# Row sums joined by 32x32 transposes on VectorE in place of products on TensorE, in a log-softmax over eight 25 KB buffers

## Chip, cores, metric

One core of one Trainium2 chip. The metric is device time in microseconds of one execution. All runs quoted here are on record as of the fast state, with a granted clock of 1.0.

## The reference

```python
# x: (16, 512, 50000) float32
max_x = np.max(x, axis=-1, keepdims=True)
shifted = x - max_x
log_sum_exp = np.log(np.sum(np.exp(shifted), axis=-1, keepdims=True))
return (shifted - log_sum_exp).astype(np.float32)
```

## The kernel before

A tile is 16 rows. Each row is cut into G = 8 pieces of 6250 numbers, one piece per partition, so a tile is 128 x 6250 float32: 25 KB per partition, 3125 KB in all. There are 512 tiles and eight buffers, used in turn. Since a row lies on eight partitions, its maximum and its sum have to be joined over those eight. The maximum was already joined by two 32x32 transposes on VectorE; the sum was joined on TensorE, by a product with a block matrix of ones.

```python
# SyncE: load tile into buffer j when the store from it is done
take(sync, stored[j])
sync.dma_start(out=bufs[j], in_=dram(xq, q, j)).then_inc(landed[j], 16)

# VectorE, per tile: front(j), then back(j - 1)
def front(j):
    take(vector, landed[j])
    vector.reduce_max(out=pmax, in_=bufs[j], axis=AX)            # 128x6250
    # transpose, reduce over groups of 8, spread, transpose back -> shift[j]
    ...
def back(j):                                                     # waits for logs[j]
    vector.tensor_scalar(out=bufs[j], in0=bufs[j], scalar1=shift[j][:, 0:1],
                         scalar2=logs[j], op0=ALU.add, op1=ALU.subtract)

# ScalarE, per tile: front(j), then back(j - 1)
def front(j):
    for c in range(nexp):                                        # 2 exponentials, waiting for shift[j]
        scalar.activation(out=dump, ..., func=ACT.Exp, accum_out=parts[j][:, c:c+1])
    added.next(scalar.activation(out=logs[j], in_=rowsum[:, j:j+1], func=ACT.Ln))
def back(q, j):                                                  # waits for the subtract of j
    subtracted.next(scalar.dma_start(out=dram(oq, q, j), in_=bufs[j]))

# TensorE, per tile: both partial sums, joined over the partitions of a row
for c in range(nexp):
    tensor.matmul(rowsum[:, j:j+1], ones, parts[j][:, c:c+1], start=c == 0, stop=c == nexp - 1)
```

(Semaphores are cut here except where a name shows which wait is meant.)

Of the kernel before, what the change touches and what calls it, by code (L numbers as in the profile page):

```python
# [8 lines left out]
FP32 = mybir.dt.float32  # L9
ACT = mybir.ActivationFunctionType  # L10
ALU = mybir.AluOpType
AX = mybir.AxisListType.X

P = 128
SQ = 32

G = 8
R = P // G
# [22 lines left out]
def take(engine, sem):  # L41

    engine.wait_ge(sem, 16).then_inc(sem, -16)  # L43


@with_exitstack
def kernel(
    ctx: ExitStack,
    tc: tile.TileContext,
    x: bass.AP,  # L50
    out: bass.AP,
):
    nc = tc.nc
    xf = x.flatten_outer_dims()
    of = out.flatten_outer_dims()
    N, V = xf.shape
    W = V // G
    assert N % R == 0 and V % G == 0 and W % EXP_C == 0
    ntiles = N // R
    nexp = W // EXP_C  # L60
    assert ntiles % NBUF == 0 and ntiles >= 2 * NBUF

    rounds = ntiles // NBUF
    xq = xf.rearrange("(q j r) (g w) -> q j (r g) w", j=NBUF, r=R, g=G)
    oq = of.rearrange("(q j r) (g w) -> q j (r g) w", j=NBUF, r=R, g=G)

    data = ctx.enter_context(tc.tile_pool(name="data", bufs=1))
    stats = ctx.enter_context(tc.tile_pool(name="stats", bufs=1))
    consts = ctx.enter_context(tc.tile_pool(name="consts", bufs=1))
    dump_pool = ctx.enter_context(  # L70
        tc.tile_pool(name="dump", bufs=1, space=bass.MemoryType.PSUM)
    )
    sum_pool = ctx.enter_context(
        tc.tile_pool(name="sums", bufs=1, space=bass.MemoryType.PSUM)
    )

    ones = consts.tile([P, P], FP32)
    bufs = [data.tile([P, W], FP32, name=f"buf{j}") for j in range(NBUF)]
    shift = [stats.tile([P, SQ], FP32, name=f"negmax{j}") for j in range(NBUF)]
    logs = [stats.tile([P, 1], FP32, name=f"logsum{j}") for j in range(NBUF)]  # L80
    parts = [stats.tile([P, nexp], FP32, name=f"part{j}") for j in range(NBUF)]
    pmax = stats.tile([P, 1], FP32, name="pmax")
    allmax = stats.tile([P, SQ], FP32, name="allmax")
    rowmax = stats.tile([P, SQ // G], FP32, name="rowmax")
    spread = stats.tile([P, SQ], FP32, name="spread")
    dump = dump_pool.tile([P, EXP_C], FP32, name="dump")
    rowsum = sum_pool.tile([P, NBUF], FP32, name="rowsum")


    ctx.enter_context(tc.tile_critical())  # L90

    def sem(name):
        return ctx.enter_context(nc.semaphore(name))

    landed = [sem(f"landed{j}") for j in range(NBUF)]
    stored = [sem(f"stored{j}") for j in range(NBUF)]
    ready = sem("ones_ready")
    on_dve = Count(sem("on_dve"))
    on_act = Count(sem("on_act"))
    shifted = Count(sem("shifted"))  # L100
    summed = Count(sem("summed"))
    added = Count(sem("added"))
    logged = Count(sem("logged"))
    subtracted = Count(sem("subtracted"))


    def dram(a, q, j):
        if isinstance(q, int):
            return a[q, j]
        return a[bass.ds(q, 1), j].rearrange("o p w -> (o p) w")  # L110

    block = ctx.enter_context(nc.Block())

    @block.gpsimd
    def _(gpsimd):

        ones3 = ones.rearrange("p (r g) -> p r g", g=G)
        gpsimd.memset(ones, 1.0).then_inc(ready)  # L118
        gpsimd.affine_select(  # L119
            out=ones3, in_=ones3, pattern=[[-G, R], [0, G]], base=0,  # L120
            channel_multiplier=1, compare_op=ALU.is_ge, fill=0.0,
        ).wait_op(ready, 1, "sem-ge").then_inc(ready)
        gpsimd.affine_select(  # L123
            out=ones3, in_=ones3, pattern=[[G, R], [0, G]], base=G - 1,
            channel_multiplier=-1, compare_op=ALU.is_ge, fill=0.0,
        ).wait_op(ready, 2, "sem-ge").then_inc(ready)

    @block.sync
    def _(sync):
        for j in range(NBUF):  # L130
            sync.dma_start(out=bufs[j], in_=dram(xq, 0, j)).then_inc(landed[j], 16)
        with sync.Fori(1, rounds) as q:
            for j in range(NBUF):
                take(sync, stored[j])
                sync.dma_start(out=bufs[j], in_=dram(xq, q, j)).then_inc(landed[j], 16)
        for j in range(NBUF):
            take(sync, stored[j])

    @block.vector
    def _(vector):  # L140
        def front(j):
            take(vector, landed[j])
            vector.reduce_max(out=pmax, in_=bufs[j], axis=AX).then_inc(on_dve.sem)  # L143

            on_dve.next(
                vector.transpose(out=allmax, in_=pmax.to_broadcast([P, SQ]))  # L146
            ).then_inc(on_dve.sem)
            on_dve.next(
                vector.tensor_reduce(  # L149
                    out=rowmax, in_=allmax.rearrange("p (r g) -> p r g", g=G),  # L150
                    op=ALU.max, axis=AX, negate=True,
                )
            ).then_inc(on_dve.sem)
            on_dve.next(
                vector.tensor_copy(  # L155
                    out=spread.rearrange("p (r g) -> p r g", g=G),
                    in_=rowmax[:, :, None].to_broadcast([P, SQ // G, G]),
                )
            ).then_inc(on_dve.sem)
            on_dve.next(vector.transpose(out=shift[j], in_=spread)).then_inc(shifted.sem)  # L160

        def back(j):
            logged.next(
                vector.tensor_scalar(  # L164
                    out=bufs[j], in0=bufs[j], scalar1=shift[j][:, 0:1], scalar2=logs[j],
                    op0=ALU.add, op1=ALU.subtract,
                )
            ).then_inc(subtracted.sem)

        def settle():  # L170
            on_dve.settle(vector)
            logged.settle(vector)

        for j in range(NBUF):
            front(j)
            if j:
                back(j - 1)
        settle()
        with vector.Fori(1, rounds):
            for j in range(NBUF):  # L180
                front(j)
                back((j - 1) % NBUF)
            settle()
        back(NBUF - 1)

    @block.scalar
    def _(scalar):
        def front(j):
            for c in range(nexp):
                ins = scalar.activation(  # L190
                    out=dump, in_=bufs[j][:, c * EXP_C : (c + 1) * EXP_C], func=ACT.Exp,
                    bias=shift[j][:, 0:1], scale=1.0, accum_out=parts[j][:, c : c + 1],
                )
                (on_act if c else shifted).next(ins)
                ins.then_inc(on_act.sem if c < nexp - 1 else summed.sem)
            added.next(
                scalar.activation(out=logs[j], in_=rowsum[:, j : j + 1], func=ACT.Ln)  # L197
            ).then_inc(logged.sem)

        def back(q, j):  # L200
            subtracted.next(
                scalar.dma_start(out=dram(oq, q, j), in_=bufs[j])
            ).then_inc(stored[j], 16)

        def settle():
            for count in (on_act, shifted, added, subtracted):
                count.settle(scalar)

        nc.scalar.preload_act_table_set("natural_log_exp_and_others")  # L209
        for j in range(NBUF):  # L210
            front(j)
            if j:
                back(0, j - 1)
        settle()
        with scalar.Fori(1, rounds) as q:
            last = q - 1
            for j in range(NBUF):
                front(j)
                back(q if j else last, (j - 1) % NBUF)
            settle()  # L220
        back(rounds - 1, NBUF - 1)

    @block.tensor
    def _(tensor):
        def add(j):
            for c in range(nexp):
                ins = tensor.matmul(  # L227
                    rowsum[:, j : j + 1], ones, parts[j][:, c : c + 1],
                    start=c == 0, stop=c == nexp - 1,
                )  # L230
                if c == 0:
                    summed.next(ins)
            ins.then_inc(added.sem)

        tensor.wait_ge(ready, 3)
        with tensor.Fori(0, rounds):
            for j in range(NBUF):
                add(j)
            summed.settle(tensor)


# [28 lines left out]
```

## Time and profile before

| | before |
|---|---|
| time, median of the 3 runs known at first | 7620.1 us |
| steady period of a tile | 14.87 us |
| bytes moved in the steady part | 432 GB/s |
| VectorE / ScalarE / TensorE busy | 73% / 41% / 7% |
| a load, issue to landing; a store | 51.8 us; 37.0 us |

How to read the page: "DMA" gives the busy share of the 16 DMA engines in 40 equal slices of the run, in tenths, and "GB/s" what they moved in each. A line of a group is: source line, engine, operation, output and inputs, shapes, count | busy us in all, mean ns of one | idle us of that engine just before them, and what ended it. A line of a timeline is: start us, duration us, engine, and so on, with the idle time before it in brackets. The lines themselves, from the page and from one steady cycle, stand in the prediction.

### The profile page before, as it was taken

The page shows a single profiled execution, that of the slowest core. Times are in us where ns is not written, and L with a number is a line of the kernel's source. Part 1 is how long each engine was busy: PE and PEld are TensorE (multiplying, and loading weights), DVE is VectorE, ACT ScalarE, POOL GpSimd, SP SyncE. Part 2 cuts the span into 40 slices and gives each one's busy share as a digit, 9 for nine tenths or more (in the row PEclk, how much of TensorE's full clock was granted, in tenths as well). Part 3 has the DMA queues.
Part 4 walks back from the last instruction along what each step waited for, and adds up shares of the span by engine and source line. Part 5 has one row for each costly group of instructions (what it writes and reads, how often), then busy time and mean ns, then how long its engine had stood idle before and what let it go on. Part 6 is the DMA issues. An engine that isn't in the chain of part 4 may idle for free. (4 is left out here: it accounts for less than half of the span.)

```text
span 7617.7 us, 14954 instructions
## 1 busy us (share of the span) xinstructions
PE 519.0 (7%) x2048; PEld 475.1 (6%) x2048; DVE 5565.8 (73%) x3072; ACT 3153.3 (41%) x2561; POOL 1.2 (0%) x7
## 2 busy tenths in 40 slices
PE   0000000000000000000000000000000000000000
PEld 0000000000000000000000000000000000000000
DVE  7777777777777777777777777777777777777776
ACT  4444444444444444444444444444444444444443
POOL 0000000000000000000000000000000000000000
DMA  9999999999999999999999999999999999999998
GB/s 424 432 433 432 432 432 432 433 432 432 432 433 433 432 432 432 433 432 432 432 432 433 432 432 432 433 433 432 431 432 433 432 432 432 432 432 432 431 430 366
DMA packets 147459, 3276.88 MB, mean 430 GB/s; under 512 B 16385, under 2 KB 16385, under 8 KB 16385
## 3 DMA queue, kind: packets, MB, share of 16 engines
q1 hardware_dynamic: 73728, 1638.43, 50.0%
q10 hardware_dynamic: 73728, 1638.43, 50.0%
q14 instruction: 3, 0.02, 0.0%
HBM read 1638.40 MB, written 1638.40 MB: 430 GB/s over the span
## 5 line engine op out<-in xcount | busy, mean ns | idle before, releaser
L143 DVE TENSOR_REDUCE pmax<-buf 128x1 f32<-128x6250 f32 x512 | 3411.5, 6663 | 1960.6 <-DVEq L43 1960.6
L190 ACT ACTIVATE dump<-buf,negmax 128x3125 f32<-128x3125 f32 x1024 | 2938.2, 2869 | 3878.6 <-DVE negmax L160 3862.1
L164 DVE TENSOR_SCALAR buf<-buf,negmax,logsum 128x6250 f32<-128x6250 f32 x512 | 1789.4, 3495 | 3.9 <-ACT logsum L197 3.9
L227 PE MATMUL rowsum<-part,ones 128*128 128x1 f32 x2048 | 519.0, 357 | 7078.5 <-ACT dump L190 7078.5
L227 PEld LDWEIGHTS rowsum<-part,ones 128*128 128x128 f32 x2048 | 475.1, 322 | 7122.2 <-ACT dump L190 7122.2
L197 ACT ACTIVATE logsum<-rowsum 128x1 f32<-128x1 f32 x512 | 87.6, 171 | 564.8 <-PE rowsum L227 564.8
L190 ACT ACTIVATION_READ_ACCUMULATOR dump<-buf,negmax 128x1 f32 x1024 | 190.8, 186 | 0.0
L160 DVE STREAM_TRANSPOSE negmax<-spread 128x32 f32<-128x32 f32 x512 | 108.3, 212 | 17.7
L146 DVE STREAM_TRANSPOSE allmax<-pmax 128x32 f32<-128x32 f32 x512 | 108.3, 211 | 17.6
L149 DVE TENSOR_REDUCE rowmax<-allmax 128x4 f32<-128x32 f32 x512 | 95.1, 186 | 17.7
L155 DVE COPY spread<-rowmax 128x32 f32<-128x32 f32 x512 | 92.5, 181 | 17.8
L209 ACT ACT_TABLE_LOAD x1 | 1.3, 1283 | 1.0 <-SPq L90 1.0
L119 POOL TENSOR_SCALAR_AFFINE_SELECT ones<-ones 128x128 f32<-128x128 f32 x1 | 0.4, 403 | 0.1
L123 POOL TENSOR_SCALAR_AFFINE_SELECT ones<-ones 128x128 f32<-128x128 f32 x1 | 0.4, 397 | 0.1
L118 POOL MEMSET ones<- 128x128 f32 x1 | 0.2, 204 | 0.5 <-SPq L90 0.5
L254 POOL MEMSET const-bfloat16-1.0<- 128x1 bf16 x1 | 0.1, 101 | 0.0
L254 POOL MEMSET const-uint8-127<- 128x1 uint8 x1 | 0.1, 101 | 0.0
L254 POOL MEMSET const-float32-0.0<- 128x1 f32 x1 | 0.1, 98 | 0.3 <-issue 0.3
L254 POOL MEMSET const-float32-1.0<- 128x1 f32 x1 | 0.1, 98 | 0.0
## 6 DMA issues: line engine op xcount, KB each, us to landing
buf<-in_x_dram SPq DMA_DIRECT2D x512, 3125.0 KB, 51.8
out_dram<-buf ACTq DMA_DIRECT2D x512, 3125.0 KB, 37.0
```

The costliest lines, as they stand in the source:

```text
L119: gpsimd.affine_select(out=ones3, in_=ones3, pattern=[[-G, R], [0, G]], base=0, channel_multiplier=1, compare_op=ALU.is_ge, fill=0.0,).wai ...
L123: gpsimd.affine_select(out=ones3, in_=ones3, pattern=[[G, R], [0, G]], base=G - 1, channel_multiplier=-1, compare_op=ALU.is_ge, fill=0.0,) ...
L143: vector.reduce_max(out=pmax, in_=bufs[j], axis=AX).then_inc(on_dve.sem)
L146: vector.transpose(out=allmax, in_=pmax.to_broadcast([P, SQ]))
L149: vector.tensor_reduce(out=rowmax, in_=allmax.rearrange("p (r g) -> p r g", g=G), op=ALU.max, axis=AX, negate=True,)
L155: vector.tensor_copy(out=spread.rearrange("p (r g) -> p r g", g=G), in_=rowmax[:, :, None].to_broadcast([P, SQ // G, G]),)
L160: on_dve.next(vector.transpose(out=shift[j], in_=spread)).then_inc(shifted.sem)
L164: vector.tensor_scalar(out=bufs[j], in0=bufs[j], scalar1=shift[j][:, 0:1], scalar2=logs[j], op0=ALU.add, op1=ALU.subtract,)
L190: ins = scalar.activation(out=dump, in_=bufs[j][:, c * EXP_C : (c + 1) * EXP_C], func=ACT.Exp, bias=shift[j][:, 0:1], scale=1.0, accum_out ...
L197: scalar.activation(out=logs[j], in_=rowsum[:, j : j + 1], func=ACT.Ln)
L209: nc.scalar.preload_act_table_set("natural_log_exp_and_others")
L227: ins = tensor.matmul(rowsum[:, j : j + 1], ones, parts[j][:, c : c + 1], start=c == 0, stop=c == nexp - 1,)
```

## The change

The intent: the join of the sums leaves TensorE. VectorE adds the two partial sums and sends them through the same four small operations that join the maximum (now a helper, `share`), just before the subtract that needs them. So that ScalarE does not stop for this, its logarithm of tile j-1 is moved ahead of the exponentials of tile j.

```diff
     def _(vector):
-        def front(j):
-            take(vector, landed[j])
-            vector.reduce_max(out=pmax, in_=bufs[j], axis=AX).then_inc(on_dve.sem)
+        def share(out, op, done, negate=False):
             ... (transpose, reduce by groups of 8, spread, transpose back: as before)
+        def front(j):
+            take(vector, landed[j])
+            vector.reduce_max(out=own, in_=bufs[j], axis=AX).then_inc(on_dve.sem)
+            share(shift[j], ALU.max, shifted, negate=True)

         def back(j):
+            summed.next(
+                vector.tensor_reduce(out=own, in_=parts[j], op=ALU.add, axis=AX)
+            ).then_inc(on_dve.sem)
+            share(totals[j], ALU.add, added)
             logged.next(
                 vector.tensor_scalar(
... (ScalarE)
+        def log(j):
             added.next(
-                scalar.activation(out=logs[j], in_=rowsum[:, j : j + 1], func=ACT.Ln)
+                scalar.activation(out=logs[j], in_=totals[j][:, 0:1], func=ACT.Ln)
             ).then_inc(logged.sem)
...
             for j in range(NBUF):
+                log((j - 1) % NBUF)
                 front(j)
                 back(q if j else last, (j - 1) % NBUF)
             settle()
+        log(NBUF - 1)
         back(rounds - 1, NBUF - 1)
-
-    @block.tensor
-    ... (all of it, and GpSimd's making of the matrix of ones)
```

More of the change, by code (lines that the diff above doesn't have):

```diff
@@ L68 @@
     stats = ctx.enter_context(tc.tile_pool(name="stats", bufs=1))
-    consts = ctx.enter_context(tc.tile_pool(name="consts", bufs=1))
     dump_pool = ctx.enter_context(
@@ L72 @@
     )
-    sum_pool = ctx.enter_context(
-        tc.tile_pool(name="sums", bufs=1, space=bass.MemoryType.PSUM)
-    )
-    ones = consts.tile([P, P], FP32)
     bufs = [data.tile([P, W], FP32, name=f"buf{j}") for j in range(NBUF)]
     shift = [stats.tile([P, SQ], FP32, name=f"negmax{j}") for j in range(NBUF)]
+    totals = [stats.tile([P, SQ], FP32, name=f"total{j}") for j in range(NBUF)]
     logs = [stats.tile([P, 1], FP32, name=f"logsum{j}") for j in range(NBUF)]
     parts = [stats.tile([P, nexp], FP32, name=f"part{j}") for j in range(NBUF)]
-    pmax = stats.tile([P, 1], FP32, name="pmax")
-    allmax = stats.tile([P, SQ], FP32, name="allmax")
-    rowmax = stats.tile([P, SQ // G], FP32, name="rowmax")
+    own = stats.tile([P, 1], FP32, name="own")
+    block32 = stats.tile([P, SQ], FP32, name="block32")
+    rowval = stats.tile([P, SQ // G], FP32, name="rowval")
     spread = stats.tile([P, SQ], FP32, name="spread")
     dump = dump_pool.tile([P, EXP_C], FP32, name="dump")
-    rowsum = sum_pool.tile([P, NBUF], FP32, name="rowsum")
     ctx.enter_context(tc.tile_critical())
@@ L96 @@
     stored = [sem(f"stored{j}") for j in range(NBUF)]
-    ready = sem("ones_ready")
     on_dve = Count(sem("on_dve"))
@@ L112 @@
     block = ctx.enter_context(nc.Block())
-    @block.gpsimd
-    def _(gpsimd):
-        ones3 = ones.rearrange("p (r g) -> p r g", g=G)
-        gpsimd.memset(ones, 1.0).then_inc(ready)
-        gpsimd.affine_select(
-            out=ones3, in_=ones3, pattern=[[-G, R], [0, G]], base=0,
-            channel_multiplier=1, compare_op=ALU.is_ge, fill=0.0,
-        ).wait_op(ready, 1, "sem-ge").then_inc(ready)
-        gpsimd.affine_select(
-            out=ones3, in_=ones3, pattern=[[G, R], [0, G]], base=G - 1,
-            channel_multiplier=-1, compare_op=ALU.is_ge, fill=0.0,
-        ).wait_op(ready, 2, "sem-ge").then_inc(ready)
     @block.sync
@@ L140, in _ @@
     def _(vector):
-        def front(j):
-            take(vector, landed[j])
-            vector.reduce_max(out=pmax, in_=bufs[j], axis=AX).then_inc(on_dve.sem)
+        def share(out, op, done, negate=False):
             on_dve.next(
-                vector.transpose(out=allmax, in_=pmax.to_broadcast([P, SQ]))
+                vector.transpose(out=block32, in_=own.to_broadcast([P, SQ]))
             ).then_inc(on_dve.sem)
@@ L149, in front @@
                 vector.tensor_reduce(
-                    out=rowmax, in_=allmax.rearrange("p (r g) -> p r g", g=G),
-                    op=ALU.max, axis=AX, negate=True,
+                    out=rowval, in_=block32.rearrange("p (r g) -> p r g", g=G),
+                    op=op, axis=AX, negate=negate,
                 )
@@ L156, in front @@
                     out=spread.rearrange("p (r g) -> p r g", g=G),
-                    in_=rowmax[:, :, None].to_broadcast([P, SQ // G, G]),
+                    in_=rowval[:, :, None].to_broadcast([P, SQ // G, G]),
                 )
             ).then_inc(on_dve.sem)
-            on_dve.next(vector.transpose(out=shift[j], in_=spread)).then_inc(shifted.sem)
+            on_dve.next(vector.transpose(out=out, in_=spread)).then_inc(done.sem)
+        def front(j):
+            take(vector, landed[j])
+            vector.reduce_max(out=own, in_=bufs[j], axis=AX).then_inc(on_dve.sem)
+            share(shift[j], ALU.max, shifted, negate=True)
         def back(j):
+            summed.next(
+                vector.tensor_reduce(out=own, in_=parts[j], op=ALU.add, axis=AX)
+            ).then_inc(on_dve.sem)
+            share(totals[j], ALU.add, added)
             logged.next(
@@ L170, in settle @@
         def settle():
-            on_dve.settle(vector)
-            logged.settle(vector)
+            for count in (on_dve, summed, logged):
+                count.settle(vector)
         for j in range(NBUF):
@@ L210, in _ @@
         for j in range(NBUF):
+            if j:
+                log(j - 1)
             front(j)
@@ L220, in _ @@
             settle()
+        log(NBUF - 1)
         back(rounds - 1, NBUF - 1)
-    @block.tensor
-    def _(tensor):
-        def add(j):
-            for c in range(nexp):
-                ins = tensor.matmul(
-                    rowsum[:, j : j + 1], ones, parts[j][:, c : c + 1],
-                    start=c == 0, stop=c == nexp - 1,
-                )
-                if c == 0:
-                    summed.next(ins)
-            ins.then_inc(added.sem)
-        tensor.wait_ge(ready, 3)
-        with tensor.Fori(0, rounds):
-            for j in range(NBUF):
-                add(j)
-            summed.settle(tensor)
 _INS = ['x']
```

## The prediction

The sums stand as they were forecast; a term of them is what the reduce of the two partial sums takes. VectorE's added 0.95 us a tile (512 x 0.95 = 486 us in all, to about 6050) is 0.79 us by the four rows of the page and, for the rest, that term; it is also in the 1.12 us of the new join with its gaps, of which 0.93 us are measured, and so in the 1.32 us by which the subtract was to start later (1.12, the logarithm's 0.17, and 0.03). The total forecast was 7620 us. At the ends, 7.4 us for a store (14.87 / 2) is an estimate from the traced period; what (b) comes to if exposed, and the factor of about three under "What will show it", are estimates from the numbers beside them.

> **What bounds the kernel now.** I read the page first, then the timeline of one steady cycle, the table of waits, and the busy time by stage. Four facts carry the reading. From the page: the DMA line, the groups of instructions, the DMA issues.
>
> ```profile
> DMA  9999999999999999999999999999999999999998
> GB/s 424 432 433 432 432 432 432 433 432 432 432 433 433 432 432 432 433 432 432 432 432 433 432 432 432 433 433 432 431 432 433 432 432 432 432 432 432 431 430 366
> ...
> L143 DVE TENSOR_REDUCE pmax<-buf 128x1 f32<-128x6250 f32 x512 | 3411.5, 6663 | 1960.6 <-DVEq L43 1960.6
> L190 ACT ACTIVATE dump<-buf,negmax 128x3125 f32<-128x3125 f32 x1024 | 2938.2, 2869 | 3878.6 <-DVE negmax L160 3862.1
> ...
> L227 PE MATMUL rowsum<-part,ones 128*128 128x1 f32 x2048 | 519.0, 357 | 7078.5 <-ACT dump L190 7078.5
> ...
> L197 ACT ACTIVATE logsum<-rowsum 128x1 f32<-128x1 f32 x512 | 87.6, 171 | 564.8 <-PE rowsum L227 564.8
> ...
> L160 DVE STREAM_TRANSPOSE negmax<-spread 128x32 f32<-128x32 f32 x512 | 108.3, 212 | 17.7
> L146 DVE STREAM_TRANSPOSE allmax<-pmax 128x32 f32<-128x32 f32 x512 | 108.3, 211 | 17.6
> L149 DVE TENSOR_REDUCE rowmax<-allmax 128x4 f32<-128x32 f32 x512 | 95.1, 186 | 17.7
> L155 DVE COPY spread<-rowmax 128x32 f32<-128x32 f32 x512 | 92.5, 181 | 17.8
> ...
> buf<-in_x_dram SPq DMA_DIRECT2D x512, 3125.0 KB, 51.8
> out_dram<-buf ACTq DMA_DIRECT2D x512, 3125.0 KB, 37.0
> ```
>
> First, the DMA line is 9 in every slice but the last and the bytes sit at 431 to 433 GB/s[...]. The busy table for 300 to 7400 us says the same: DMA share 1.00. Second, no compute engine is near that: VectorE 73%, ScalarE 41%, TensorE 7%. Third, VectorE's only large wait, 1960.6 us, is for its own queue on the semaphore that says "loaded" (DVEq): it waits for data. Fourth, a load takes 51.8 us from issue to landing although tiles land every 14.87 us (the timeline below), so 51.8 / 14.87 = 3.5 loads are queued at any time; stores likewise, 37.0 / 14.87 = 2.5. Of eight buffers six are in the DMA queues; the other two, 8 x 14.87 - 51.8 - 37.0 = 30.2 us, are in compute. The chain that ended last covers only the last tile (each line 0.1% or less), so it says nothing of the middle.
>
> The timeline of one steady cycle (start, duration, engine, line, idle before):
>
> ```profile
> 3003.35 6.67 DVE L143 TENSOR_REDUCE pmax<-buf 128x1 f32<-128x6250 f32 x1 [3.86 <-DVEq L43]
> ...
> 3010.87 3.50 DVE L164 TENSOR_SCALAR buf<-buf,negmax,logsum 128x6250 f32<-128x6250 f32 x1
> 3010.98 2.87 ACT L190 ACTIVATE dump<-buf,negmax 128x3125 f32<-128x3125 f32 x1 [7.57 <-DVE negmax L160]
> ...
> 3017.05 1.01 PE L227 MATMUL rowsum<-part,ones 128*128 128x1 f32 x4 [13.85 <-ACT dump L190]
> 3018.10 0.17 ACT L197 ACTIVATE logsum<-rowsum 128x1 f32<-128x1 f32 x1 [1.10 <-PE rowsum L227]
> 3018.23 6.66 DVE L143 TENSOR_REDUCE pmax<-buf 128x1 f32<-128x6250 f32 x1 [3.86 <-DVEq L43]
> 3018.24 0.34 ACTq L202 DMA_DIRECT2D out_dram<-buf  x1
> ```
>
> The line to see is the last: ScalarE issues the store of the previous tile only after its logarithm of this one (3018.24), though the subtract had ended at 3010.87 + 3.50 = 3014.37. The store waits in ScalarE's program order, not for VectorE.
>
> [...]loads and stores here share 432 GB/s, 50.0% each in the queue table. [...]
>
> **The change part by part, per tile.**
>
> Removed: four matmuls, 1.01 us on TensorE, with the wait that ScalarE had for them, 564.8 / 512 = 1.10 us. TensorE and GpSimd fall silent. That lies on the path from the exponentials to the logarithm, but that path does not set the period.
>
> Added on VectorE, ahead of the subtract: one reduce of the two partial sums[...]; then a second copy of the join: 211 + 186 + 181 + 212 = 790 ns by its four rows. Busy: 0.95 us per tile, 512 x 0.95 = 486 us in all, so VectorE goes from 5565.8 to about 6050 us, 79%. In time: the present join takes from 3010.05 (its first transpose) to 3010.98 (ScalarE released), 0.93 us with gaps[...]. Then the logarithm, 0.17 us, and about 0.03 us to release the subtract: it starts 1.32 us later than now. VectorE's idle time ahead of each row maximum falls from 3.86 to about 2.5 us; it is still idle, so it cannot become the bound.
>
> Moved: the logarithm of tile j-1 goes ahead of the exponentials of tile j on ScalarE. The exponentials, which now start at 3010.98, start 1.21 us later, at 3010.87 + 1.12 + 0.20 = 3012.19. They take 6.02 us with their accumulator reads (3010.98 to the matmuls' start at 3017.05 with release), so they end at 3018.21, and the store, next in program order and with its subtract done at 3012.19 + 3.50 = 3015.69, is issued at about 3018.25. Before: 3018.24. **The two delays cancel**: 1.1 us for the matmuls and 0.17 for the logarithm leave the end of ScalarE's cycle, about 1.2 us of waiting for the join and the same logarithm come in at its start. A buffer is held as long as before, to 0.1 us.
>
> Ends: the loads of the first eight buffers are issued at once and the DMA is already at 422 to 430 GB/s from 10 us on, while VectorE works off a backlog at 10.9 us a tile. That pace becomes about 10.9 + 1.3 = 12.2 us, still under 14.87, so the backlog lasts longer but the queues stay full: no loss. The last tile: the last chain grows by 1.3 us (last subtract from 7597.66 to about 7598.95), but the store before it is still issued at about 7597.6, since it too follows exponentials, and two stores of 7.4 us each (14.87 / 2) then run one behind the other; the last joins the queue at 7602.5 instead of 7601.2, before the first is done at 7605. So 0 to 0.2 us. Sum: 7620.1 + 0 to 0.5.
>
> **The rivals.** (a) *VectorE's added 486 us shows in the time*: 7620 + 486 = 8106, +6.4%. For it: VectorE is the busiest compute engine and the work goes there serially. Against: 3.86 us idle per tile to hold 1.32. (b) *A later store starves the loads*: if the cancellation fails and each store goes out 1.3 us later, a buffer's stay in the queues shrinks from 88.8 to 87.5 us of the 119. Against it being felt: it takes the loss of all but about one queued load, 51.8 - 14.87 = 37 us, before the load queue runs dry (an estimate). Even fully exposed in the cycle of eight buffers it is 1.3 / 8 = 0.16 us a tile, 84 us, 1.1%: 7704. (c) *The shorter path makes it faster*: TensorE and its 1.10 us wait go. Against: at 432 GB/s the 3276.88 MB need 7585 us, and only 33 us of the 7617.7 lie outside that[...]. (d) *A different logarithm*: it reads SBUF, not PSUM, and alternates with the exponential otherwise; the exponential's table set is loaded once (one ACT_TABLE_LOAD on the page), and both are already served from it.[...]
>
> **Range and chances.** The DMA bound does not move, and both path changes fall in slack. I predict 7620 us. The three runs before spread 2.3 us; chip to chip and the phase of the two queues I allow 8 to 10 us either way: 7611 to 7630. Same 98%; 1% each for what I don't see.
>
> **What will show it.** In the profile after: DMA at 9 throughout and 431 to 433 GB/s; VectorE near 6050 us busy; its wait for loads down from 3.86 to about 2.5 us a tile; a new ScalarE wait of about 8.6 us a tile ahead of the logarithm, hardly any ahead of the exponentials; no TensorE; landing times still near 52 and 37 us; stores issued about 14.9 us after the row maximum starts. It would be wrong if the small VectorE operations cost several times their rows (2.5 us of slack would go at about three times), or if the GB/s line fell below 430 with VectorE still waiting for loads.

## The result, and the profile after

The changed kernel takes 7614.07 us (median of 6 runs, 7613.84 to 7614.37) against 7618.7 us of the kernel before (median of 6, 7617.62 to 7620.4). The ratio is 0.9994, with a 95% interval of 0.9981 to 1.0006: the same. Ratios are the mean time of one kernel's fast runs over that of the other's of the same rounds, so not quite the ratio of the medians quoted.

The page after, with the lines that answer to those of the prediction:

```profile
DVE 6049.3 (79%) x5632; ACT 3113.4 (41%) x2561; POOL 0.2 (0%) x4
...
DMA  9999999999999999999999999999999999999998
GB/s 425 432 432 432 432 432 432 432 432 432 432 432 433 432 432 433 432 432 433 432 432 433 432 432 432 432 433 432 432 433 432 432 432 432 432 432 432 432 432 373
...
L144 DVE TENSOR_REDUCE own<-buf 128x1 f32<-128x6250 f32 x512 | 3411.7, 6663 | 1267.0 <-DVEq L43 1267.0
...
L188 ACT ACTIVATE logsum<-total 128x1 f32<-128x1 f32 x512 | 103.8, 203 | 4447.9 <-DVE total L140 4447.9
...
L149 DVE TENSOR_REDUCE own<-part 128x1 f32<-128x2 f32 x512 | 57.5, 112 | 2.4 <-ACT dump L179 2.4
...
buf<-in_x_dram SPq DMA_DIRECT2D x512, 3125.0 KB, 55.5
out_dram<-buf ACTq DMA_DIRECT2D x512, 3125.0 KB, 35.7
```

The DMA lines are as flat as before. VectorE has 483.5 us more to do (6049.3 - 5565.8), and its wait for loads has shrunk by 693.6 us (1960.6 - 1267.0): the added work, its gaps and 0.27 us of waiting for the logarithm were all taken out of time in which it waited for data. The last two lines hold a surprise: loads take 3.7 us longer to land and stores 1.3 us less, so a buffer spends 2.4 us more in the transfer queues, and 2.4 us less in compute. One steady cycle of the timeline after says why:

```profile
3003.64 6.66 DVE L144 TENSOR_REDUCE own<-buf 128x1 f32<-128x6250 f32 x1 [2.52 <-DVEq L43]
...
3011.15 0.11 DVE L149 TENSOR_REDUCE own<-part 128x1 f32<-128x2 f32 x1
...
3012.23 0.20 ACT L188 ACTIVATE logsum<-total 128x1 f32<-128x1 f32 x1 [8.77 <-DVE total L140]
3012.34 2.85 ACT L179 ACTIVATE dump<-buf,negmax 128x3125 f32<-128x3125 f32 x1
3012.46 3.54 DVE L153 TENSOR_SCALAR buf<-buf,negmax,logsum 128x6250 f32<-128x6250 f32 x1 [0.27 <-ACT logsum L188]
...
3015.34 2.87 ACT L179 ACTIVATE dump<-buf,negmax 128x3125 f32<-128x3125 f32 x1
3016.03 0.34 ACTq L193 DMA_DIRECT2D out_dram<-buf  x1
```

The subtract ends at 3012.46 + 3.54 = 3016.00, and the store is issued at 3016.03, in the middle of the second exponential (3015.34 to 3018.21). Counted from the start of the row maximum the store goes out at 12.4 us; before it was 14.9 us. The store was predicted to wait for the exponentials' end. It does not. The full trace also shows when ScalarE runs the first of the small register instructions of the store's line: 0.006 us after the start of the logarithm before (3018.106 and 3018.100), 0.006 us after the start of the second exponential now (3015.351 and 3015.345); over all the stores of the loop (504 in each trace) it is 0.005 to 0.007 us and 0.006 to 0.008 us. So in these traces it passed a running activation, but not one that was still to start; after that the store waits only for its subtract (issued 0.03 us after the subtract's end, in all 512).

Where did 5.1 us of span go (7617.7 to 7612.6)? The starts of the 512 row maxima in the two traces give three parts. The 25th starts 2.6 us later than before (344.68 against 342.09). From there to the last, 487 tiles take 5.9 us less (14.856 us a tile against 14.868). From the last one's start to the end of the span it is 33.1 us against 35.0, 1.9 us less.

The first and the last part belong together, and neither is VectorE's pace. These are the 25th row maxima of the kernel before, of the changed one, and of two kernels of the experiments below: order_only, whose VectorE has nothing added, and store_held, whose VectorE has all of the added work but whose stores go out as late as before:

```profile
342.09 6.66 DVE L143 TENSOR_REDUCE pmax<-buf 128x1 f32<-128x6250 f32 x1 [3.88 <-DVEq L43]
344.68 6.66 DVE L144 TENSOR_REDUCE own<-buf 128x1 f32<-128x6250 f32 x1 [2.45 <-DVEq L43]
345.10 6.66 DVE L143 TENSOR_REDUCE pmax<-buf 128x1 f32<-128x6250 f32 x1 [3.80 <-DVEq L43]
342.10 6.66 DVE L146 TENSOR_REDUCE own<-buf 128x1 f32<-128x6250 f32 x1 [2.53 <-DVEq L43]
```

The delay goes with the early store. Counted from the packets in the traces, all four kernels have moved the bytes of 45.6 transfers (loads and stores) by 342 us, but 25.02, 24.97, 24.88 and 25.08 of them are loads: an early store takes its turn from the loads at the start, and is not left over at the end. The two parts together are 377.1 us before, 377.8 changed, 377.1 in order_only and 377.1 in store_held. Nothing is gained there; the whole difference lies in the middle.

There the landings set the pace, not the bytes alone. A tile moves 6.40 MB, which in 14.868 us is 430.5 GB/s and not 432. In the old trace 25 loads had landed at 342 us and the bytes of 25.0 had been moved; at 7000 us 472 had landed, but the bytes of 474.9 had been moved. The transfers run ahead of the landings, and VectorE starts on a landing.

### The profile page after: what moved, and what is told of

Read it like the earlier page. It is cut to its first block, busy times and chain, and to the rows that moved or that the text cites. A ratio compares the mean times of both kernels' runs of the same rounds, so it can differ in the third digit from the quotient of the medians.

```text
span 7612.6 us, 13283 instructions
## 1 busy us (share of the span) xinstructions
DVE 6049.3 (79%) x5632; ACT 3113.4 (41%) x2561; POOL 0.2 (0%) x4
## 5 line engine op out<-in xcount | busy, mean ns | idle before, releaser
L144 DVE TENSOR_REDUCE own<-buf 128x1 f32<-128x6250 f32 x512 | 3411.7, 6663 | 1267.0 <-DVEq L43 1267.0
L188 ACT ACTIVATE logsum<-total 128x1 f32<-128x1 f32 x512 | 103.8, 203 | 4447.9 <-DVE total L140 4447.9
L153 DVE TENSOR_SCALAR buf<-buf,negmax,logsum 128x6250 f32<-128x6250 f32 x512 | 1810.2, 3536 | 138.9 <-ACT logsum L188 138.9
L126 DVE STREAM_TRANSPOSE block<-own 128x32 f32<-128x32 f32 x1024 | 216.6, 212 | 35.1
L129 DVE TENSOR_REDUCE rowval<-block 128x4 f32<-128x32 f32 x1024 | 190.4, 186 | 35.4
L135 DVE COPY spread<-rowval 128x32 f32<-128x32 f32 x1024 | 185.5, 181 | 35.6
L140 DVE STREAM_TRANSPOSE total<-spread 128x32 f32<-128x32 f32 x512 | 108.4, 212 | 17.7
L149 DVE TENSOR_REDUCE own<-part 128x1 f32<-128x2 f32 x512 | 57.5, 112 | 2.4 <-ACT dump L179 2.4
## 6 DMA issues: line engine op xcount, KB each, us to landing
buf<-in_x_dram SPq DMA_DIRECT2D x512, 3125.0 KB, 55.5
```

Source lines behind the costliest of these rows:

```text
L126: vector.transpose(out=block32, in_=own.to_broadcast([P, SQ]))
L129: vector.tensor_reduce(out=rowval, in_=block32.rearrange("p (r g) -> p r g", g=G), op=op, axis=AX, negate=negate,)
L135: vector.tensor_copy(out=spread.rearrange("p (r g) -> p r g", g=G), in_=rowval[:, :, None].to_broadcast([P, SQ // G, G]),)
L140: on_dve.next(vector.transpose(out=out, in_=spread)).then_inc(done.sem)
L144: vector.reduce_max(out=own, in_=bufs[j], axis=AX).then_inc(on_dve.sem)
L149: vector.tensor_reduce(out=own, in_=parts[j], op=ALU.add, axis=AX)
```

## The experiments

The theory after this result: **the time is set by bytes, and what the change does to the path shows only in when the stores go out.** In the kernel before, the logarithm that waits for TensorE stands ahead of the store in ScalarE's program and holds it; in the changed kernel nothing that still waits stands there, so the store goes as soon as its subtract is done. Rivals: it is the absence of TensorE that counts; a later store starves the loads; VectorE's added work shows in the time. Four kernels kept eight buffers, one made VectorE too slow on purpose, and four had four buffers. The number 14.9, 12.4 and so on is always the store's issue, counted from the start of the row maximum that precedes its subtract.

### order_only: ScalarE's new order, the sums still on TensorE

```diff
+        def log(j):
             added.next(
                 scalar.activation(out=logs[j], in_=rowsum[:, j : j + 1], func=ACT.Ln)
             ).then_inc(logged.sem)
...
+                log((j - 1) % NBUF)
                 front(j)
                 back(q if j else last, (j - 1) % NBUF)
```

> The kernel before with ScalarE's order changed alone: the logarithm of tile j-1 ahead of the exponentials of tile j, the join still by products on TensorE. Theory (the 5 us come from the store's earlier issue, because ScalarE's queue can issue the store while an exponential runs once no waiting logarithm stands in front of it): the store goes out at about 11.0 us after the row maximum starts (its subtract's end), against 14.9 before and 12.4 with the whole change; loads land after more than 55.5 us; at the end the last row maximum to the end of the span takes about 31.5 us, against 35.0 before and 33.1 changed; total 7609 to 7615 us. Rival (the absence of TensorE and its products gives the 5 us): total stays at 7618 to 7620 us.

Measured: 7612.35 us (7607.33 to 7614.68, 5 runs) against 7619.49 (9 runs) of the kernel before, ratio 0.9990, interval 0.9977 to 1.0004. Its timeline:

```profile
3002.77 6.66 DVE L143 TENSOR_REDUCE pmax<-buf 128x1 f32<-128x6250 f32 x1 [3.87 <-DVEq L43]
...
3010.28 3.49 DVE L164 TENSOR_SCALAR buf<-buf,negmax,logsum 128x6250 f32<-128x6250 f32 x1
...
3013.42 2.87 ACT L190 ACTIVATE dump<-buf,negmax 128x3125 f32<-128x3125 f32 x1
3013.81 0.34 ACTq L204 DMA_DIRECT2D out_dram<-buf  x1
```

The store goes out 0.04 us after its subtract's end (3013.77), at 11.0 us, and loads take 57.3 us to land. This is the kernel before with nothing changed but an order, so the early store comes from the order and not from the join's place. The last row maximum to the end takes 7610.1 - 7578.11 = 32.0 us, near the 31.5 expected.

### store_held: the whole change, but the store held until the exponentials have ended

```diff
+        def hold(j):        # after the exponentials; runs when they have ended
+            ins = scalar.activation(out=mark, in_=parts[j][:, 0:1], func=ACT.Ln)
+            ins.then_inc(held.sem)
+            held.seen += 1
+            scalar.wait_ge(held.sem, held.seen)
...
                 front(j)
+                hold(j)
                 back(q if j else last, (j - 1) % NBUF)
```

> The changed kernel with the store held on purpose until the exponentials of the tile have ended (a small logarithm into a scratch column after them, which the store waits for). Theory (early store): the store goes out about 14.9 to 15.1 us after the row maximum starts, as in the kernel before; landing of loads falls back to about 52 us, the tail to 35 us or a little more, total back to 7618 to 7621 us. Rival (absence of TensorE): total stays at 7614 us.

Measured: 7616.76 us (7609.43 to 7617.61), ratio 0.9992, interval 0.9979 to 1.0006. Its timeline:

```profile
3002.25 6.67 DVE L146 TENSOR_REDUCE own<-buf 128x1 f32<-128x6250 f32 x1 [2.51 <-DVEq L43]
...
3011.08 3.54 DVE L155 TENSOR_SCALAR buf<-buf,negmax,logsum 128x6250 f32<-128x6250 f32 x1 [0.27 <-ACT logsum L196]
...
3016.86 0.19 ACT L189 ACTIVATE mark<-part 128x1 f32<-128x1 f32 x1
...
3017.21 0.34 ACTq L201 DMA_DIRECT2D out_dram<-buf  x1
```

The profiled run has what the theory expected of the path: the store at 15.0 us, loads landing after 51.8 us as in the kernel before, 35.0 us from the last row maximum to the end (7614.96 - 7579.95). The total missed the 7618 to 7621 expected and is inconclusive: three of its runs are at about 7617, two at 7609 to 7610. A kernel of eight buffers can thus differ by 8 us from one of its runs to the next, which is more than the 4.6 us to be explained.

The part after the last row maximum goes with the store all the same, in five traces: with the store at 11.0, 12.4, 14.9, 15.0 and 23.6 us (store_late, next) it is 32.0, 33.1, 35.0, 35.0 and 41.5 us. But the start pays it back, in store_late too (its 25th row maximum starts at 336.16 us, and the two parts are 377.7 us), so it is worth nothing in the total. The 12 ns a tile in the middle are not explained: the profiled runs have 14.868 (before), 14.862 (store_held), 14.856 (changed) and 14.852 us (order_only), which would go in the order of the store's issue; but store_late has the latest store of all and 14.862, and these are single traces of kernels with such a spread. What those 5.9 us of the middle come from stays open, and so it is not shown that the early store makes the kernel of eight buffers faster.

### store_late: each store issued only after the next tile's logarithm

```diff
                 log((j - 1) % NBUF)
+                back(q if j > 1 else last, (j - 2) % NBUF)
                 front(j)
-                back(q if j else last, (j - 1) % NBUF)
```

> The changed kernel with each store issued after the next tile's logarithm, about 11.4 us later than in the changed kernel, before any exponential of that tile. Theory (the queues hold several loads, so up to some 37 us of added holding is hidden): the bytes stay at 432 GB/s, landing of loads falls from 55.5 to about 44 us, total 7610 to 7625 us. Rival (a later store starves the loads): 11.4 us over eight buffers is 1.4 us a tile, 730 us, some 8340 us.

Measured: 7610.42 us (7608.65 to 7617.5), ratio 0.9989, interval 0.9976 to 1.0003. Its stores go out at 23.6 us, 11.2 us after their subtract's end (11.4 was expected). That hold costs nothing that shows. Loads land after 38.8 us, not 44, and stores after 41.3: the hold came out of the loads' queue (-16.7 us), part of which the stores' queue took (+5.6), and the two together lost 11.1 us. So the rival of the starved loads, some 8340 us, is out with eight buffers: what a longer hold takes away is queueing, of which there is plenty.

### joins3 and joins5: the sum's join done three and five times over

```diff
+            for _ in range(2):                      # 4 in joins5
+                share(totals[j], ALU.add, on_dve)
             share(totals[j], ALU.add, added)
```

> The changed kernel with the sum's join done three times over (two of them thrown away). Each extra join is about 0.95 us on VectorE. Theory (it fits into VectorE's 2.5 us of waiting for loads): VectorE about 6880 us busy (90%), its wait for loads 0.6 us a tile, the store 1.9 us later, total 7612 to 7620 us. Rival (VectorE work shows in the time): 7614 + 512 x 1.9 = 8590 us; also refuted if in between.

> The changed kernel with the sum's join done five times over. Four extra joins of about 0.95 us are 3.8 us, more than VectorE's 2.5 us of waiting. Theory (VectorE becomes the bound when its tile passes 14.87 us): VectorE's tile is about 12.35 + 3.8 = 16.2 us, total about 8260 to 8320 us, VectorE over 98% busy, GB/s down to about 395. Rival (the join's cost hides however large, as it overlaps transfers): 7614 us.

Measured: joins3 7626.19 us (7625.49 to 7626.94), ratio 1.0009, interval 0.9996 to 1.0023; joins5 8209.75 us, ratio 1.0776, interval 1.0758 to 1.0794. VectorE's groups that wait for loads, from the table of waits of the changed kernel, of joins3 and of joins5 (us in all, times, longest us):

```profile
DVE own L144 <- DVEq L43: 1267.0, 505, 11.3
```

```profile
DVE own L144 <- DVEq L43: 330.1, 486, 11.4
```

```profile
DVE own L144 <- DVEq L43: 11.1, 1, 11.1
```

With two joins more the wait is nearly used up (0.6 us a tile), and 1.86 us of VectorE's time a tile, 952 us in all, cost 12 us. That is 6 us above the expected range; 10 of the 12 us are in the part from the 25th to the last row maximum (14.876 us a tile against 14.856). I have no experiment on why. Its tiles are slower all along (14.870 to 14.879 us in each stretch of 60 from the 31st tile to the 390th, then 14.888 and 14.900), and towards the end its page has fewer bytes per second, which the page of the changed kernel has not:

```profile
GB/s 424 432 432 432 432 432 432 432 432 432 432 432 432 432 432 432 432 432 432 432 432 432 432 432 432 432 432 432 432 432 432 432 431 430 430 429 429 430 430 365
```

With four more VectorE never waits for a load again after its first, its tile takes 15.98 us, and the DMA falls to 400 GB/s. It is busy for 93% of the span, where I expected over 98%: most of the rest are the gaps between its small operations. The change from almost free to +7.8% comes between a VectorE tile of 14.13 us (joins3, in its first backlog) and one of 15.98 us; the period of 14.87 us lies between them. My 8260 to 8320 us were too high because a join costs 0.93 us and not 0.95, and because the changed kernel's VectorE tile, where it waits for no load, is 12.28 us (row maxima at 43.39 and 55.67 us, in its first backlog) and not 12.35: 12.28 + 4 x 0.93 = 16.00.

### Four buffers: before4, after4, order_only4, store_held4

The edit in each is NBUF = 4 in place of 8. With half the buffers there is hardly a queue to hide a hold in, so that the store's time and the join's place can be told apart: in before4, about 3000 us in, two loads took 15.7 and 16.4 us from issue to the row maximum that waited for them (2999.86 to 3015.56, 3012.83 to 3029.24), and the two stores of the same buffers just before them 16.4 and 14.6 us from issue to those loads' issue, with a period of 16.2 us (8278.97 / 512).

> The kernel before with four buffers in place of eight. A buffer is held in compute for one tile period plus 14.9 us, so of 4 x 14.87 = 59.5 us about 30 are left for a load and a store, which take about 15 to 17 us each when they share the engines. Theory: the queues run dry now and then, the period is 15 to 16.5 us, total 7700 to 8400 us. If holding time does not matter: 7620 us.

> The changed kernel with four buffers. Theory (with few buffers the holding time decides, and the changed kernel holds a buffer 2.4 us less because its store goes out earlier): faster than the kernel before with four buffers by about 2.4 / 4 = 0.6 to 2.4 / 3 = 0.8 us a tile, 300 to 400 us, if that one is starved; rival (added VectorE time makes the cycle longer): slower than it by 1.3 / 4 = 0.3 us a tile or more, 150 us.

> ScalarE's order changed alone, with four buffers. Theory (early store): the store goes out 11.0 us after the row maximum, so a buffer is held 3.9 us less than before and 1.4 us less than with the whole change: the fastest of the three, by 0.3 to 0.5 us a tile under the changed kernel with four buffers where that is starved. Rival (it is the join's place that counts): same as the kernel before with four buffers.

> The changed kernel with four buffers and the store held until the exponentials have ended, as in the kernel before. Theory (the whole difference between the two kernels with four buffers is the time of the store's issue): back to about the 8279 us of the kernel before with four buffers, 8230 to 8330 us, though there is no TensorE work. Rival (part of the 5.5% comes from the join leaving TensorE): stays well under, near 7820 to 8050 us.

| four buffers | store at | median of 4 runs | ratio to before with eight, 95% interval |
|---|---|---|---|
| before4: TensorE, old order | 14.9 us | 8278.97 us | 1.0869, 1.0848 to 1.0891 |
| store_held4: VectorE, store held | 15.0 us | 8304.98 us | 1.0897, 1.0879 to 1.0915 |
| after4: VectorE, new order | 12.4 us | 7819.89 us | 1.0260, 1.0243 to 1.0277 |
| order_only4: TensorE, new order | 11.0 us | 7726.61 us | 1.0143, 1.0126 to 1.0160 |

Here the change that does nothing with eight buffers saves 5.5% (7819.89 / 8278.97 by the medians), and the table shows what does it. With the store at its old time the kernel without TensorE is no faster than the one with it (8305 and 8279; the 26 us between them, measured on two different chips, I did not pursue; the intervals overlap). A tile of store_held4:

```profile
3992.51 6.66 DVE L146 TENSOR_REDUCE own<-buf 128x1 f32<-128x6250 f32 x1 [2.77 <-DVEq L43]
...
4001.34 3.54 DVE L155 TENSOR_SCALAR buf<-buf,negmax,logsum 128x6250 f32<-128x6250 f32 x1 [0.27 <-ACT logsum L196]
...
4007.48 0.34 ACTq L201 DMA_DIRECT2D out_dram<-buf  x1
```

With the new order the kernel with TensorE is faster still, and its store goes out 1.4 us earlier. after4's gain, 459 us or 0.90 us a tile, is a little over the 0.6 to 0.8 expected; order_only4's further 0.18 us a tile is less than the expected 0.3 to 0.5. That its 15.09 us a tile are already close to 14.87 may be why; no run tests it. The busy table for 300 to 7400 us of each (VectorE, ScalarE; clock, DMA share, GB/s at the end), first of before4 and then of after4:

```profile
300.00:7400.00 7100.00, 445.17 (x1756) 407.64 (x1756) 4777.49 (x2635) 2702.54 (x2196) 0.00 (x0) 1.00 0.97 396
```

```profile
300.00:7400.00 7100.00, 5498.18 (x5117) 2830.24 (x2329) 0.00 (x0) 1.00 1.00 420
```

(The first has two columns of TensorE ahead of VectorE.) The share of busy time hardly tells them apart, 0.97 and 1.00; the bytes do, 396 and 420 GB/s against 432. So the engines were hardly ever without work: the mean packet of 25,000 bytes took 978 ns in before4 and 954 in after4, against 929 in the kernel before with eight buffers, and that is most of the shortfall. Why packets take longer with four buffers stays open; that the loss follows the store's issue is what the four runs show.

## Why the prediction was right, and where it was not

- **The bound.** Right: the DMA moves 432 GB/s before and after; only joins5 and the runs with four buffers fell clearly below, and only they became slower by over 1%. The flat DMA line alone did not show it, though: joins5's page has a 9 in every slice but the last too, at about 400 GB/s, and there VectorE sets the pace. What shows it is that joins3's work and store_late's hold hardly cost anything.
- **VectorE's cost.** Right in the sum: 6049.3 us busy against about 6050, waits for loads 2.5 us a tile against about 2.5. Two terms were off and cancelled: the reduce of two partial sums took 112 ns, where the sum left 0.16 us for it (0.95 - 0.79), and the subtract, 3536 ns and not 3495. (At the last tile, behind 2.37 us of idle time, the reduce took 150 ns, one instruction.) Its start after the first join came 1.31 us later (3012.46 - 3011.15), against 1.32.
- **The two delays cancel.** Wrong. This step put the store "next in program order" after the exponentials, at 3018.25 in the old trace's time, 14.9 us. It went out at 12.4 us, when its subtract was done. The old trace could have told: its store came 0.14 us after the start of the logarithm, the first moment at which nothing ahead of it waited any more, and I took that for the end of ScalarE's cycle. order_only and store_held show both sides.
- **A buffer is held as long as before.** Wrong for the same reason: 2.4 us less, so landing rose to 55.5 us, where about 52 was named.
- **The ends.** I forecast 0 to 0.2 us more at the end and no loss at the start. Both come from the store, which was put too late: by the row maxima the end took 1.9 us less and the start 2.6 us more, together 0.7 us more.
- **The rivals.** (a) is refuted by joins3, and true only past the edge that joins5 shows. (b) is refuted for eight buffers by store_late; with four, a later store did cost time, though the engines hardly ran dry. (c), the absence of TensorE, is refuted for four buffers by store_held4; its sum, only 33 us outside the transfers, took 432 GB/s for the pace of the tiles, which is 430.5 (512 x 14.868 = 7612 us). (d): the logarithm takes 203 ns against 171. In (b) the 84 us should be 83.

The outcome was 5.9 us from the number forecast and inside the range, because the failed step concerned a hold that eight buffers hide; rival (b) had named that slack, by estimate 37 us, of which store_late's hold used 11.2. That the time fell by 4.6 us was not forecast, and its cause stays open. With four buffers the same error would have meant a forecast of no change where the chip gives 5.5%.

## What to carry to other kernels

Ask first how deep the transfer queues are (time from issue to landing, over the period of a tile): with 3.5 tiles queued, a shorter path and a longer one cost nearly the same here, while no engine's tile passed the period; with about one queued (before4: 15.7 and 16.4 us over 16.2), the store's time decided. The store issued from ScalarE was late because an instruction ahead of it still waited (it went 3.87 us after its subtract's end in the kernel before, 0.04 us in order_only); where two instructions can change places, put the one that waits after the store. The order alone, with TensorE kept, was the best with four buffers and, within the spread, as good as any with eight: the join on VectorE buys nothing here but a silent TensorE.
